# A decoder block on one core: scaling before the transpose in the second half, and reloads of merged tokens on ScalarE's DMA queue

## The chip, the cores and the metric

One core of a Trainium2 chip runs the whole kernel. The metric is the device time of one execution in microseconds (us). Three runs of the kernel before gave 3618.96, 3622.24 and 3625.21 us; their median is 3622.24 us.

## The reference, cut to what matters

The input is 512 tokens of 2048 channels, all in f32. The block computes two mixers, joins them, and ends in an expert layer:

```python
xn = rmsnorm(x, norm_mix)
proj = xn @ w_in                       # 2048 -> 10240: conv, attention and gate parts
merged = sigmoid(g_conv) * (y_conv @ w_conv_out) + sigmoid(g_attn) * (y_attn @ w_attn_out)
x = x + merged @ w_out                 # 2048 x 2048
xn = rmsnorm(x, norm_ffn)              # x * rsqrt(mean(x^2) + eps) * gain
q = xn @ peer_wq                       # queries of 8 heads, then top-16 of the keys
x = x + peer_ffn(xn, ...)              # 128 experts' rows of u and v per token
return rmsnorm(x, norm_final)
```

The change touches two places: how the merged tokens get back on chip ahead of `merged @ w_out`, and how the second `rmsnorm` is turned into the transposed operand of `xn @ peer_wq`.

## The kernel before, in words

**Halves of numbers.** TensorE multiplies f32 data as three products: every operand is split into a high half (a copy rounded by ScalarE, L133) and a low half (source minus high half, by VectorE, L134). `split` does both. `mm3` (L164 to L166) issues the three matmuls: high by high, high by low, low by high. Weights come from HBM in raw pieces of 128 x 1024 (512 KB, `whalf`, L148, on SyncE's DMA queue, called SP). Four raw buffers (`wraw`) and three buffers each of halves (`whi`, `wlo`) are in rotation.

**Token halves.** The 512 tokens are worked on as two halves of 256, h = 0 and h = 1. For each half `mixer` runs the projections, attention and convolution, then 16 blocks of the merge (block d = 0 to 15; each takes two raw pieces of `w_mix`, 24 matmuls a piece, 48 a block). Merged blocks 0 to 12 are parked in HBM (`md`), because their place on chip is still taken by the normalised input `xhi`, `xlo`. After the last projection has read that input, eight DMAs bring the parked blocks back into the same place (L345 to L348: for each of four groups of blocks a high and a low part; six DMAs of 512 KB and two of 128 KB). Blocks 13, 14 and 15 are merged after that and go there directly. `outproj` then multiplies by `w_out`, adds the residual, and takes the sum of squares of each row (L484, L485).

**The chain.** `chain` makes the second normalisation and the transposed operand of the query projection. It takes the inverse root mean square of each of two token tiles (`rms_inv`, L197 to L199, one number per token), broadcasts it along the other axis by a small matmul (L499, L500, L503: the tile `cinv`), transposes the two row tiles `x2` in eight pairs of 128-column blocks (`turn`, four transposes into one PSUM buffer of three, L208), multiplies each transposed block by gain and `cinv` into SBUF (L509, VectorE, twice a pair), and splits the pair (512 columns) into the halves `nhi`, `nlo`. For h = 1 it also reloads the 64 token columns left over from h = 0 (`ntd`, L525, L526). `queries` (L535 on) follows and needs what the chain gives.

**What sets the order.** The code is traced in program order; a list scheduler then orders each engine's instructions, taking by program order what is ready by its own estimate. [...] Beside the second half runs a gather: GpSimd fetches rows of `u` and `v` by index (L691, about 1 MB each, on its own DMA queue), and VectorE consumes them (L702, L709).

Of the kernel before, what the change touches and what calls it, by code (L numbers as in the profile page):

```python
# [8 lines left out]
F32 = mybir.dt.float32  # L9
# [3 lines left out]
AF = mybir.ActivationFunctionType  # L13
OP = mybir.AluOpType
# [4 lines left out]
P = 128  # L19
T = 512  # L20
D = 2048
KD = D // P
NH = 256
# [9 lines left out]
G0 = P + NG2  # L33
# [20 lines left out]
XKB = 3  # L54
# [12 lines left out]
PINT = 1  # L67
# [13 lines left out]
def block_kernel(ctx, tc, a, out, dbg=None):  # L81
    nc = tc.nc
# [22 lines left out]
    gffn = const.tile([P, KD], F32, name="gffn")  # L105
# [7 lines left out]
    xn2d = dram.tile([G0, D], F32, name="xn2d")  # L113
    kd = dram.tile([NPAIR, P, NH], F32, name="kd")
    vd = dram.tile([NPAIR, P, 2, P], F32, name="vd")
    md = dram.tile([2, 2, P, KD, NH], F32, name="md")
    ntd = dram.tile([2, P, KD, NH - G0], F32, name="ntd")
# [6 lines left out]
    def row():  # L124
        return late[0].tile([P, D], F32, name="row", bufs=ROWS)
# [6 lines left out]
    def split(src, hi, lo):  # L132
        nc.scalar.activation(hi, src, AF.Copy)  # L133
        nc.vector.tensor_tensor(lo, src, hi.bitcast(F32), OP.subtract)  # L134
# [24 lines left out]
    def behind(ins):  # L159

        tc.add_manual_dep(ins.ins, pe_last[0].ins.name, mybir.DependencyInfo(mybir.DependencyClass.NoSync, mybir.DependencyReason.DATA), reason="behind")
# [15 lines left out]
    def accum():  # L177
        return ps.tile([P, 512], F32, name="pj", bufs=3)
# [17 lines left out]
    def rms_inv(ss):  # L196
        nc.vector.tensor_tensor(ss[:, 0:1], ss[:, 0:1], ss[:, 1:2], OP.add)  # L197
        nc.scalar.activation(ss[:, 0:1], ss[:, 0:1], AF.Sqrt, scale=1.0 / D, bias=epst)
        nc.vector.reciprocal(ss[:, 0:1], ss[:, 0:1])  # L199
        return ss[:, 0:1]  # L200

    def turn(x2, k, pin):

        tp = accum()
        for kk in range(2):
            for tt in range(2):
                o = kk * NH + tt * P
                t = nc.tensor.transpose(tp[:, o:o + P], x2[tt][:, (k + kk) * P:(k + kk) * P + P], ident)  # L208
                if pin:
                    behind(t)  # L210
        return tp.rearrange("p (k t) -> p k t", k=2)
# [49 lines left out]
    def mixer(h, st, x):  # L261
# [67 lines left out]
        for d in range(KD):  # L329
            sg = []  # L330
            for i in (48 + d, 64 + d):
                acc = yield from project(i)
                s = mix.tile([P, NH], F32, name="sg", bufs=SG)
# [10 lines left out]
        m = st["m"] = [(st["mp"] if h == 0 else mix).tile([P, KD, NH], F32R, name=f"x{q}") for q in ("hi", "lo")]  # L344
        for k in range(0, n, 4):  # L345
            for q in range(2):
                s = slice(k, min(k + 4, n))
                nc.sync.dma_start(m[q][:, s].bitcast(F32), md[h, q, :, s])  # L348
        if h == 0:
            st["x1"] = load_x(1)  # L350
        while todo:
# [139 lines left out]
    def chain(pool, h, box, nhi, nlo, c0):  # L491

        x2 = box["x2"]
        ib = accum()
        rns = []
        for tt in range(2):
            rn = rms_inv(box["ssq"][tt])
            rb = pool.tile([P, P], F32, name="rb", bufs=2)
            nc.scalar.mul(rb, ones, rn)  # L499
            nc.tensor.matmul(ib[:, tt * P:tt * P + P], rb, ident, start=True, stop=True)  # L500
            rns.append(rn)
        inv = pool.tile([P, NH], F32, name="cinv", bufs=1)
        nc.scalar.copy(inv, ib[:, 0:NH])  # L503
        yield
        for k in range(0, KD, 2):
            tp = turn(x2, k, h == 0 and PINT)
            xk = pool.tile([P, 2, NH], F32, name="sg", bufs=1 if h == 0 else XKB)
            for j in range(2):
                nc.vector.scalar_tensor_tensor(xk[:, j], tp[:, j], gffn[:, k + j:k + j + 1], inv, OP.mult, OP.mult)  # L509
            split(xk, nhi[:, k:k + 2, c0:c0 + NH], nlo[:, k:k + 2, c0:c0 + NH])  # L510
            yield
        if h == 0:
            grow = row()
            nc.sync.dma_start(grow, a["norm_ffn"].broadcast_to([P, D]))
            yield
            for tt, rn in enumerate(rns):
                xn = x2[tt]
                nc.vector.scalar_tensor_tensor(xn, xn, rn, grow, OP.mult, OP.mult)
                stop = min(tt * P + P, G0)
                nc.sync.dma_start(xn2d[tt * P:stop], xn[0:stop - tt * P])  # L520
                yield
            nc.sync.dma_start(ntd[0], nhi[:, :, G0:].bitcast(F32))
            nc.sync.dma_start(ntd[1], nlo[:, :, G0:].bitcast(F32))
        else:
            nc.sync.dma_start(nhi[:, :, 0:c0].bitcast(F32), ntd[0])  # L525
            nc.sync.dma_start(nlo[:, :, 0:c0].bitcast(F32), ntd[1])  # L526

    def queries(pool, h, st, nhi, nlo, c0):

# [409 lines left out]
    box = [{}, {}]  # L939
    with tc.tile_pool(name="mp", bufs=1) as st["mp"]:  # L940
        for _ in mixer(0, st, load_x(0)):
            pass
        for _ in outproj(sm, 0, st["m"], box[0]):
            pass
    ahead = mixer(1, st, st["x1"])
    n0 = [mix.tile([P, KD, NH], F32R, name=n) for n in ("yhi", "ylo")]
    ch = chain(sm, 0, box[0], *n0, 0)
    for i in range(6):
        next(ahead)
# [43 lines left out]
    with tc.tile_pool(name="cp", bufs=1, side="right") as cp:  # L993
        for _ in chain(cp, 1, box[1], *st["dense_x"], ND - NH):
            pass
# [98 lines left out]
```

## Time and profile before

| | |
|---|---|
| the profiled execution's own time | 3618.28 us |
| its span | 3616.6 us |
| mean granted TensorE clock | 0.991 of full speed |
| VectorE busy | 2832.1 us (78%) |
| ScalarE busy | 1618.0 us (45%) |
| GpSimd busy | 654.8 us (18%) |
| SyncE's and ScalarE's DMA queue together (q1) | 649.38 MB, all of it issued by SP |
| GpSimd's DMA queue (q0) | 402.68 MB |

"Busy" is the share of the span in which an engine has an instruction running; matmuls overlap, so a busy TensorE is not one at its peak. In the rows further down, PE is TensorE, PEld its weight load, ACT ScalarE, DVE VectorE, SPq the issuing of DMAs by SyncE. A view by time gives for each row the start in us, the length in us, engine, line and operation, with output and inputs by the program's names; in square brackets stands how long the engine had been idle before it and what it had waited for.

### The profile page before, as it was taken

How to read it: one execution, taken by the hardware profiler on the slowest of the kernel's cores; microseconds unless marked ns; L12 is line 12 of the kernel's file. 1: busy time of each engine (PE TensorE's matmuls, PEld its weight loads, DVE VectorE, ACT ScalarE, POOL GpSimd, SP SyncE). 2: the span in 40 equal slices, each digit the busy share in tenths (PEclk: the TensorE clock that was granted, in tenths of full speed). 3: DMA queues.
4: the chain of work that ended last, by engine and by line, in shares of the span. 5: the costliest groups of instructions: out<-in, count | busy, mean ns of one | idle time of the engine just before them, and what ended most of it. 6: DMA issues, size and time to landing. Idle time of an engine off the chain costs nothing.

```text
span 3616.6 us, 63343 instructions
## 1 busy us (share of the span) xinstructions
PE 3515.7 (97%) x25347; PEld 3410.5 (94%) x25347; DVE 2832.1 (78%) x4022; ACT 1618.0 (45%) x2275; POOL 654.8 (18%) x520
## 2 busy tenths in 40 slices
PE   9999999999999999889999999999999999999998
PEld 8999998898888999779999999999999999999997
DVE  6665557559987888788999886888887888888885
ACT  5454445445555544544337763333333333333334
POOL 0000000001333222112131111221122322322220
PEclk9999999999999999999999999999999999999998
DMA  5556666654788999898888889899988988899884
GB/s 195 178 180 227 214 213 218 202 191 135 265 347 316 339 353 337 328 331 330 309 319 325 316 307 367 330 351 341 337 333 319 360 326 337 325 338 348 324 321 149
DMA packets 297815, 1056.10 MB, mean 292 GB/s; under 512 B 36464, under 2 KB 109296, under 8 KB 243568
## 3 DMA queue, kind: packets, MB, share of 16 engines
q1 hardware_dynamic: 242224, 649.38, 51.5%
q0 software_dynamic: 55296, 402.68, 28.7%
q8 instruction: 199, 3.26, 0.4%
q14 instruction: 96, 0.79, 0.1%
HBM read 999.98 MB, written 51.38 MB: 291 GB/s over the span
## 4 chain that ended last, share of the span: by engine, by line
PE 58%; DVE 4%; DMA 3%; issue 1%; ACT 1%; SPq 0%; POOL 0%; ACTq 0%; DVEq 0%
PE pj L166 10%; PE pj L164 9%; PE pj L165 9%; PE z L164 9%; PE z L165 9%; PE z L166 9%; PE pj L674 2%; DVE wlo L134 2%; DMA wraw<-in_w_in 1%; DMA row<-in_v,idx 0%; DVE row L702 0%; DMA wraw<-in_w_mix 0%; DMA gt<-gd 0%; DMA hb<-hdd 0%; DVE row L709 0%
## 5 line engine op out<-in xcount | busy, mean ns | idle before, releaser
L133 ACT ACTIVATE whi<-wraw 128x1024 fp32r<-128x1024 f32 x827 | 874.1, 1059 | 1241.2 <-PE pj L165 708.1
L134 DVE TENSOR_TENSOR wlo<-wraw,whi 128x1024 fp32r<-128x1024 f32 x827 | 1007.0, 1221 | 409.1 <-ACT whi L133 401.5
L166 PE MATMUL pj<-xhi,wlo 128*128 128x256 f32 x2560 | 720.5, 283 | 14.2 <-DVE wlo L134 13.8
L164 PE MATMUL pj<-xhi,whi 128*128 128x256 f32 x2560 | 721.8, 282 | 9.4 <-ACT whi L133 7.3
L165 PE MATMUL pj<-xlo,whi 128*128 128x256 f32 x2560 | 717.6, 281 | 0.0
L164 PE MATMUL pj<-dxhi,whi 128*128 128x320 f32 (+1 forms) x2304 | 710.3, 309 | 5.0 <-ACT whi L133 4.9
L166 PE MATMUL pj<-dxhi,wlo 128*128 128x320 f32 (+1 forms) x2304 | 703.8, 307 | 3.1 <-DVE wlo L134 2.9
L165 PE MATMUL pj<-dxlo,whi 128*128 128x320 f32 (+1 forms) x2304 | 705.4, 306 | 0.0
L164 PE MATMUL z<-ahi,whi 128*128 128x320 f32 x2048 | 632.7, 310 | 3.9 <-ACT z L193 2.9
L165 PE MATMUL z<-alo,whi 128*128 128x320 f32 x2048 | 633.1, 310 | 2.4 <-DVE alo L134 2.4
L166 PE MATMUL z<-ahi,wlo 128*128 128x320 f32 x2048 | 630.8, 310 | 1.8 <-DVE wlo L134 1.8
L166 PEld LDWEIGHTS pj<-xhi,wlo 128*128 128x128 f32 x2560 | 480.6, 188 | 24.3 <-DVE wlo L134 20.9
L164 PEld LDWEIGHTS pj<-xhi,whi 128*128 128x128 f32 x2560 | 481.6, 188 | 17.0 <-ACT whi L133 10.6
L165 PEld LDWEIGHTS pj<-xlo,whi 128*128 128x128 f32 x2560 | 481.4, 188 | 2.5 <-issue 1.4
L691 POOL DMA_INDIRECT row<-in_v,idx x192 | 288.5, 1503 | 1064.9 <-DVE row L709 412.3
L709 DVE SCALAR_TENSOR_TENSOR row<-row,gact 128x2048 f32<-128x2048 f32 x192 | 450.1, 2345 | 26.6 <-DMA row<-in_v,idx 26.3
L702 DVE SCALAR_TENSOR_TENSOR row<-row,gx 128x2048 f32<-128x2048 f32 x192 | 438.3, 2286 | 32.2 <-DMA row<-in_u,idx 32.2
L691 POOL DMA_INDIRECT row<-in_u,idx x192 | 289.7, 1509 | 859.1 <-DVE row L702 251.3
L164 PEld LDWEIGHTS pj<-dxhi,whi 128*128 128x128 f32 x2304 | 434.4, 189 | 6.3 <-ACT whi L133 5.9
L166 PEld LDWEIGHTS pj<-dxhi,wlo 128*128 128x128 f32 x2304 | 433.0, 188 | 5.1 <-DVE wlo L134 5.1
L165 PEld LDWEIGHTS pj<-dxlo,whi 128*128 128x128 f32 x2304 | 434.1, 188 | 0.0
L133 ACT ACTIVATE whi<-spare 128x1024 fp32r<-128x1024 f32 x197 | 208.9, 1060 | 422.4 <-PE z L165 257.6
(232 smaller groups left out, 4987.0 us busy)
## 6 DMA issues: line engine op xcount, KB each, us to landing
wraw<-in_w_in SPq DMA_DIRECT2D x320, 512.0 KB
wraw<-in_uT SPq DMA_DIRECT2D x187, 512.0 KB
wraw<-in_vT SPq DMA_DIRECT2D x128, 512.0 KB
spare<-in_vT SPq DMA_DIRECT2D x128, 512.0 KB
spare<-in_uT SPq DMA_DIRECT2D x69, 512.0 KB
wraw<-in_w_mix SPq DMA_DIRECT2D x64, 512.0 KB
wraw<-in_w_out SPq DMA_DIRECT2D x64, 512.0 KB
wraw<-in_wq SPq DMA_DIRECT2D x64, 512.0 KB
```

What stands on the lines that cost most here:

```text
L133: nc.scalar.activation(hi, src, AF.Copy)
L134: nc.vector.tensor_tensor(lo, src, hi.bitcast(F32), OP.subtract)
L164: nc.tensor.matmul(acc, shi, mhi, start=first, stop=False)
L165: nc.tensor.matmul(acc, shi, mlo, start=False, stop=False)
L166: pe_last[0] = nc.tensor.matmul(acc, slo, mhi, start=False, stop=last)
L674: behind(nc.tensor.matmul(gp[:, t * P:t * P + P], oh[:, t, 0], oh[:, t, 1], start=True, stop=True))
L691: ins = nc.gpsimd.indirect_dma_start(out=g, out_offset=None, in_=tab, in_offset=bass.IndirectOffsetOnAxis(ap=idx[0:np_, s:s + 1], axis=0))
L702: pin(nc.vector.scalar_tensor_tensor(g, g, 1.0, gx, OP.mult, OP.mult, accum_out=hid[:, s:s + 1]))
L709: pin(nc.vector.scalar_tensor_tensor(acc[0:np_], g, act[:, s:s + 1], acc[0:np_], OP.mult, OP.add))
```

## The change

For h = 1 three things differ. The eight reloads of `md` are issued by ScalarE instead of SyncE. The chain scales the rows first (`xs`, a new tile per token tile; ScalarE the left 1024 columns, VectorE the right 1024), transposes the scaled rows, and makes high and low half straight from PSUM, 256 columns at a time, with the gain as a per-partition number; the broadcast matmul, `cinv` and the tile `xk` are gone for h = 1. And the `ntd` reloads stand at the head of the chain in program order instead of at its end. For h = 0 nothing is changed but the nesting of the code.

```diff
-                nc.sync.dma_start(m[q][:, s].bitcast(F32), md[h, q, :, s])
+                (nc.scalar if h else nc.sync).dma_start(m[q][:, s].bitcast(F32), md[h, q, :, s])
...
     def chain(pool, h, box, nhi, nlo, c0):
         x2 = box["x2"]
+        if h:
+            nc.sync.dma_start(nhi[:, :, 0:c0].bitcast(F32), ntd[0])
+            nc.sync.dma_start(nlo[:, :, 0:c0].bitcast(F32), ntd[1])
+            xs = []
+            for tt in range(2):
+                rn = rms_inv(box["ssq"][tt])
+                xs.append(pool.tile([P, D], F32, name="xs", bufs=2))
+                nc.scalar.activation(xs[tt][:, :1024], x2[tt][:, :1024], AF.Copy, scale=rn)
+                nc.vector.tensor_scalar(xs[tt][:, 1024:], x2[tt][:, 1024:], rn, None, OP.mult)
+            yield
+            for k in range(0, KD, 2):
+                tp = turn(xs, k, False)
+                for j in range(2):
+                    g = gffn[:, k + j:k + j + 1]
+                    hi, lo = (t[:, k + j, c0:c0 + NH] for t in (nhi, nlo))
+                    nc.scalar.activation(hi, tp[:, j], AF.Copy, scale=g)
+                    nc.vector.scalar_tensor_tensor(lo, tp[:, j], g, hi.bitcast(F32), OP.mult, OP.subtract)
+                yield
+            return
         ib = accum()
...
-            tp = turn(x2, k, h == 0 and PINT)
-            xk = pool.tile([P, 2, NH], F32, name="sg", bufs=1 if h == 0 else XKB)
+            tp = turn(x2, k, PINT)
+            xk = pool.tile([P, 2, NH], F32, name="sg", bufs=1)
...
-        else:
-            nc.sync.dma_start(nhi[:, :, 0:c0].bitcast(F32), ntd[0])
-            nc.sync.dma_start(nlo[:, :, 0:c0].bitcast(F32), ntd[1])
```

## Rows read from the trace of the kernel before

**Rows 1.** The page: busy time of TensorE, its share and instructions.

```profile
PE 3515.7 (97%) x25347; PEld 3410.5 (94%) x25347; DVE 2832.1 (78%) x4022; ACT 1618.0 (45%) x2275; POOL 654.8 (18%) x520
```

**Rows 2.** Chain that ended last, 1430 to 1640: start, length, work.

```profile
1448.31 7.41 DMA xlo<-md
1455.78 15.80 DMA wraw<-in_w_mix
```

**Rows 3.** TensorE by time, the last merge blocks and the start of outproj.

```profile
1448.23 0.28 PE L164 MATMUL pj<-yhi,whi 128*128 128x256 f32 x1
...
1462.37 0.49 PE L646 MATMUL tr<-ident,eg 128*128 128x128 f32 x3
1472.71 0.58 PE L164 MATMUL pj<-yhi,whi 128*128 128x256 f32 x1 [9.86 <-ACT whi L133]
...
1478.84 1.25 PE L674 MATMUL pj<-spare 128*128 128x128 f32 x8
1479.84 0.51 PE L164 MATMUL z<-whi,xhi 128*128 128x512 f32 x1
```

**Rows 4.** A stretch: us, busy us of five engines, clock, DMA share, GB/s.

```profile
1465.00:1470.00 5.00, 0.00 (x0) 0.00 (x0) 3.29 (x7) 1.66 (x5) 0.94 (x1) 0.56 1.02 409
```

**Rows 5.** DMA issues by SP, in order of time.

```profile
1440.09 5.94 SPq L148 DMA_DIRECT2D wraw<-in_w_mix  x4
1448.31 0.33 SPq L348 DMA_DIRECT2D xlo<-md  x1
...
1454.04 0.32 SPq L348 DMA_DIRECT2D xlo<-md  x1
```

**Rows 6.** SP's waits, 1430 to 1500: waited for, us in total, times, longest.

```profile
SPq L148 <- DMA xlo<-md: 2.5, 2, 1.4
...
SPq L348 <- DMA wraw<-in_w_mix: 1.3, 1, 1.3
```

**Rows 7.** ScalarE by time, two pieces of weights.

```profile
1448.31 1.06 ACT L133 ACTIVATE whi<-wraw 128x1024 fp32r<-128x1024 f32 x1 [1.77 <-PE pj L165]
...
1476.00 1.06 ACT L133 ACTIVATE whi<-wraw 128x1024 fp32r<-128x1024 f32 x1 [2.07 <-DMA wraw<-in_w_out]
```

**Rows 8.** TensorE by time, from the end of outproj to the queries.

```profile
1583.44 0.39 PE L166 MATMUL z<-whi,xlo 128*128 128x512 f32 x1
...
1590.94 1.91 PE L208 MATMUL pj<-ident,row 128*128 128x128 f32 x8
...
1600.49 0.36 PE L164 MATMUL pj<-dxhi,whi 128*128 128x256 f32 x1 [0.16 <-DVE sg L509]
```

**Rows 9.** Stretches of the chain, columns as in rows 4.

```profile
1588.00:1590.00 2.00, 0.00 (x0) 0.00 (x0) 2.00 (x7) 1.26 (x4) 1.33 (x1) 0.62 0.83 243
...
1594.00:1596.00 2.00, 2.00 (x12) 1.59 (x11) 2.00 (x6) 1.19 (x2) 0.00 (x0) 0.68 0.95 377
```

**Rows 10.** VectorE by time in the chain.

```profile
1589.60 0.15 DVE L199 RECIPROCAL ssq<-ssq 128x1 f32<-128x1 f32 x1
1589.67 2.27 DVE L702 SCALAR_TENSOR_TENSOR row<-row,gx 128x2048 f32<-128x2048 f32 x1
...
1591.87 0.15 DVE L199 RECIPROCAL ssq<-ssq 128x1 f32<-128x1 f32 x1
1593.75 2.44 DVE L509 SCALAR_TENSOR_TENSOR sg<-pj,gffn,cinv 128x256 f32<-128x256 f32 x6 [1.73 <-ACT cinv L503]
```

**Rows 11.** Groups by line, 1430 to 1640: busy us, mean ns, idle before.

```profile
L134 DVE TENSOR_TENSOR wlo<-wraw,whi 128x1024 fp32r<-128x1024 f32 x57 | 69.2, 1221 | 31.9 <-ACT whi L133 31.8
...
L134 DVE TENSOR_TENSOR dxlo<-sg,dxhi 128x512 fp32r<-128x512 f32 x8 | 5.3, 683 | 0.1
```

**Rows 12.** Single lines elsewhere with like forms: minimum, median, maximum ns.

```profile
L900 ACT ACTIVATE row<-row,rn x3: 1135/1148/1149, 3605.7 to 3609.0; 128x1024 f32<-128x1024 f32 x2, 64x1024 f32<-64x1024 f32 x1
L902 DVE TENSOR_SCALAR row<-row,rn x3: 745/753/754, 3605.2 to 3609.0; 128x1024 f32<-128x1024 f32 x2, 64x1024 f32<-64x1024 f32 x1
L235 ACT ACTIVATE xhi<-row,gmix x16: 492/493/507, 8.1 to 19.4; 128x256 fp32r<-128x256 f32 x16
```

More of the change, by code (lines that the diff above doesn't have):

```diff
@@ L511, in chain @@
             yield
-        if h == 0:
-            grow = row()
-            nc.sync.dma_start(grow, a["norm_ffn"].broadcast_to([P, D]))
-            yield
[L516 to L523, printed above, removed]
-        else:
-            nc.sync.dma_start(nhi[:, :, 0:c0].bitcast(F32), ntd[0])
-            nc.sync.dma_start(nlo[:, :, 0:c0].bitcast(F32), ntd[1])
+        grow = row()
+        nc.sync.dma_start(grow, a["norm_ffn"].broadcast_to([P, D]))
+        yield
+        for tt, rn in enumerate(rns):
+            xn = x2[tt]
+            nc.vector.scalar_tensor_tensor(xn, xn, rn, grow, OP.mult, OP.mult)
+            stop = min(tt * P + P, G0)
+            nc.sync.dma_start(xn2d[tt * P:stop], xn[0:stop - tt * P])
+            yield
+        nc.sync.dma_start(ntd[0], nhi[:, :, G0:].bitcast(F32))
+        nc.sync.dma_start(ntd[1], nlo[:, :, G0:].bitcast(F32))
     def queries(pool, h, st, nhi, nlo, c0):
```

## The prediction

> **What bounds the kernel now.** I read the page first: TensorE is busy 97% of the span and no other engine comes near [rows 1]. So only time in which TensorE stands still, or runs slow, can be won, and both edits sit at such a place. The chain of waits shows the first: between two stretches of matmuls the end is set by a reload of merged tokens (7.41 us) and then by the load of one raw piece of `w_mix` (15.80 us) that stood behind it on SP [rows 2]. TensorE by time shows the price: it runs five pieces of the last merge blocks from 1448.23 to 1462.37, 2.83 us a piece, stands idle 9.86 us for the sixth, and then takes 1478.84 - 1472.71 = 6.13 us for it instead of 2.83 [rows 3]. The stretches say why: the granted clock falls while it waits (mean 0.56 in the stretch without a matmul, so on the lower level, 1.2 GHz, about 3 us after the idling began), with the DMA engines full at 409 GB/s [rows 4]. If the sixth piece had been there, 9.86 + 6.13 - 2.83 = 13.2 us would be saved. That is the ceiling of the first edit.
>
> The second place is the chain: TensorE does its last matmul of the output projection at 1583.44 and its first of the queries at 1600.49 [rows 8], 17 us later, with only transposes in between.
>
> **First edit: the reloads on ScalarE's queue.** Why did the sixth piece come late? SP issues strictly in order: five pieces of `w_mix` are out, then come the eight reloads from 1448.31 to 1454.36 [rows 5], then the sixth piece at 1455.78. It waited until the first reload had landed (1448.31 + 7.41 = 1455.72), and the eighth reload had waited 1.3 us for a piece of `w_mix` [rows 6]: counted in order of issue, each DMA waits for the one eight places before it. Then the piece was behind 3 MB of reloads: from 1455.72 to 1471.58, 15.86 us, the queue landed seven reloads and the piece, 5 x 512 + 2 x 128 + 512 KB = 3.4 MB, 215 GB/s. That is half of the 409 GB/s [rows 4]; the gather has the other half.
>
> With the reloads issued by ScalarE, the sixth piece has only one piece ahead of it on SP. No row shows a DMA issued by ScalarE, nor three queues at work. Bounds: the queues share evenly (a third each, 136 GB/s, 3.9 us for 512 KB), or nothing is won and the piece still lands at 1471.58. I take thirds, as two queues shared in halves. Even if the piece must still wait for the first reload, it goes out by 1455.7 and lands after at most two pieces' time, 1463.5: about when TensorE asks for it (1462.86).
>
> What the move costs is on ScalarE. It executes in order too, so the eight issues and their waits now stand in front of its other work. They become ready when TensorE has read the last of the input, at the same moment as the split of the fourth-last piece (first of block 14, 1448.31 in [rows 7]), and they are earlier in program order, so I expect all eight ahead of it. Behind them on ScalarE: that split, two more, and a sigmoid that nobody needs soon. TensorE gets to that piece at 1448.23 + 2 x 2.83 = 1453.89. Lower end of the cost: the eight places are not shared, the issues take 8 x 0.5 = 4 us, ScalarE is free at 1452.4, the high half is there at 1453.5 and the low half 1.2 us later [rows 11]: under 1 us. Upper end: the last reload waits for a landing as before, 1454.36, and that landing, with three queues instead of two, is up to 2.3 us later: 1456.7 + 1.06 + 1.22 = 1459, 5 us. I take 3.5. I take it without a fall of the clock, which needed about 3 us of idling at this place [rows 4] and 5 us after the output projection (0.62 in the stretch from 1588 [rows 9]); a fall would cost another 3.3.
>
> What is late next? The output projection needs two pieces of `w_out` and the first two reloads. In the trace the second such piece was split at 1476.00 [rows 7]; the queue had then landed some 5.9 MB since 1448.31. At two thirds of 409 GB/s the same bytes take 21.7 us: 1470.0, and the new start would be 1479.84 - 13.2 + 3.5 = 1470.1. So nearly nothing is lost there; I put 0.7 us. First edit: -13.2 + 3.5 + 0.7 = -9.0.
>
> The Trainium skill speaks against this edit: "DMA: Bandwidth & Descriptors", section "Issuing engines are not separate DMA queues", says that DMAs started by several engines run on the same 16 DMA engines and interleave, and that issuing from several saves only the sequencer's time. The full DMA share at this place [rows 4] agrees with one set of engines; whether an interleaved third goes to the piece that TensorE waits for, no row shows. Its result is the second rival.
>
> **Second edit: scale, transpose, split.** Taken from VectorE per pair: one subtraction of 512 columns (683 ns) [rows 11]. Old cost of a pair on VectorE: 2 x 2.44/6 = 0.81 [rows 10] plus 0.65 = 1.46 us. New cost: two fused operations of the same form, 0.81 us. ScalarE per pair: one of 512 columns becomes two of 256, 0.49 each alone [rows 12], less what neighbours overlap, 0.8 to 0.98. TensorE: the same 32 transposes, 0.24 each at the lower clock, 0.96 a pair (1.91 for eight [rows 8]). So a pair costs 0.85 to 0.96 instead of 1.46.
>
> But the start is later. Before, three pairs were transposed while the root was still being worked out. Now the scaling must come first: the second inverse root is ready at 1592.02, late because a gather row of 2.27 us sits between the two reciprocals [rows 10]; I leave it there. ScalarE's half row takes 1.15 us, VectorE's 0.75 [rows 12] beside it: 1593.2. First pair transposed at 1594.2, its halves done at 1595.6 (0.45 + 0.48 + 0.41 and small waits). The queries start when a PSUM buffer comes free, at the end of the sixth pair, as in [rows 8], where VectorE's L509 released it: 1595.6 + 5 x 0.85 to 0.96 = 1599.9 to 1600.4, against 1600.49. Gain: 0.1 to 0.6; I take 0.3. Ends: with the gather row out of the way -2.6; with it in the middle of the pairs +2.0; if the clock, low at 1588 and high again at about 1595 under transposes [rows 9], wakes only under the queries, +3.3 more (the size of [rows 3]). The reloads of `ntd` went out as soon as their place was free, and still do: nothing. The removed broadcast matmuls and `cinv` are inside the 1592.02 to 1593.75 that the scaling replaces [rows 10].
>
> **Sum.** -9.0 - 0.3 = -9.3 us. The profiled execution took 3618.3, 4.0 below the median of the runs, so the sum gives 3609.0 on its own base and 3612.9 on the median's. I predict 3611, between them.
>
> **Rivals** (times on the base of 3620.3, midway as well).
> - *ScalarE is not held up.* The eight places are counted for each queue alone, or the scheduler puts the splits first. For it: ScalarE is busy only 45% of the span [rows 1]. Against it: program order. The first edit gives 13.2 - 0.7: 3620.3 - 12.8 = 3607.5.
> - *The bytes bound it.* The same bytes must land before the output projection can start, whoever issues them; if the third queue takes its share from SP and not from the gather, the second `w_out` piece still lands at 1476.0, and the projection starts at about 1477 instead of 1479.84, perhaps without the slow clock: -3, 3617. For it: the DMA share of 1.02 [rows 4]; against it: the even split seen between two queues. This is the skill's rule carried through.
> - *ScalarE held until the reloads land (slower).* If ScalarE's queue takes new DMAs only as earlier ones land, at 3.9 us a piece, it is free at t, and TensorE idles from 1453.89 to t + 2.3 and pays 3.3 for the clock. Against the 13.2 of today this breaks even at t = 1461.5 and costs over 0.2% from t = 1468.7. With five of the eight waiting so, t = 1448.3 + 5 x 3.9 + 4 = 1472: +10.5, 3631. For it: the eighth reload did wait for a landing [rows 6]. Against it: on SP seven did not.
> - *The chain turns worse.* The gather row amid the pairs and the clock down: +5.3 instead of -0.3, 3616.6.
>
> **Chances.** Forecast 0.42, first rival 0.18, bytes 0.16, slower 0.12, chain 0.12. A change of 0.2% (7 us) is about what a measurement of this kernel can tell from none. Faster by more: the first rival whole and four fifths of the forecast, since a fall of the clock would take it below the bound: 0.53. Slower by more: the slower case, less its milder half, and some for an order of instructions that moves elsewhere: 0.11. Between: 0.36. The range goes from the first rival, with the lower base and 2 us for its gather row, 3603, to just above the chain case and the bytes on the median's base, 3622.
>
> **What would show it.** Right: the idle time of 9.86 us before the sixth piece is gone and its matmuls run at 2.83 us; an idle time of 2 to 5 us appears before the first piece of block 14, waiting for ScalarE's split; the reloads stand on ScalarE's queue from 1448 to about 1455; the output projection starts near 1470. In the chain: VectorE 0.8 to 0.95 us a pair, first transpose after 1593 on this clock of events, queries within a microsecond of before. Wrong: the sixth piece still lands after 1468, ScalarE's split of block 14 comes after 1461, or the transposes run at the lower clock into the queries. The later stages should be shifted only; a change of over 3 us after the queries would come from another order of instructions, which I have not priced.

## The result: slower by half a per cent, and the profile after

The changed kernel took 3640.47 us (median; 3639.17 to 3646.62), the kernel before 3622.84 us beside it (3618.96 to 3625.21). The ratio is 1.0054, 95% interval 1.0042 to 1.0066: 17.6 us more, where 9.3 less was predicted. The profiled execution took 3639.24 us (span 3637.5, mean granted clock 0.987 against 0.991).

Both kernels split the same 1024 weight pieces in the same sequence (ScalarE, L133), so the start of the i-th split says how far each is (the piece numbers below count from 0 in this sequence). This table gives by how much a profile fell behind the profile of the kernel before in each part, in us. The last row but one is the edit of the chain alone, the last the edit of the reloads alone (both are experiments below).

| | up to the last projection (1438) | to outproj, under way (1512) | to its end (1573) | chain, to the queries (1625) | queries, first dense pieces (1785) | to 1813 | to 2005 | to the end |
|---|---|---|---|---|---|---|---|---|
| after | 4.3 | 0.6 | 0.0 | 3.4 | 0.1 | 6.2 | 4.5 | 2.0 |
| after, run again | 5.9 | 3.5 | 0.0 | 3.5 | 0.8 | 8.9 | 1.9 | 4.6 |
| chain alone | 7.9 | -2.8 | 0.0 | 2.6 | 0.0 | 0.0 | -0.4 | -0.3 |
| reloads alone | 4.0 | 3.7 | 0.0 | 0.2 | -0.2 | 0.0 | 5.2 | -0.6 |

The first column is not the change. Up to the reloads every engine has the same instructions in the same order in all of these kernels, and the execution of the kernel before that was profiled lies 4.6 us below the median of its runs. The other columns of the first row add to 16.8 us, near the 17.6 of the medians. They name three places: the first edit won nothing (predicted: 9.0 won), the chain lost 3.4 (0.3 won), and 12.8 us were lost behind the chain, where no line was changed, 10.7 of them between 1785 and 2005.

**The first edit.** ScalarE by time, with its DMA issues (ACTq). This answers to [rows 5, 7]:

```profile
1453.03 0.34 ACTq L348 DMA_DIRECT2D xlo<-md  x1
...
1456.71 0.52 ACTq L348 DMA_DIRECT2D xhi<-md  x1
1459.40 0.33 ACTq L348 DMA_DIRECT2D xlo<-md  x1
1459.78 2.95 ACT L133 ACTIVATE whi<-wraw 128x1024 fp32r<-128x1024 f32 x3 [5.97 <-DMA xhi<-md]
1462.63 0.40 ACT L133 ACTIVATE xhi<-sg 128x256 fp32r<-128x256 f32 x1
1466.03 1.06 ACT L133 ACTIVATE whi<-wraw 128x1024 fp32r<-128x1024 f32 x1 [2.99 <-issue]
...
1479.08 0.42 ACT L133 ACTIVATE xhi<-sg 128x256 fp32r<-128x256 f32 x1 [0.71 <-DVE sg L317]
1479.40 2.93 ACT L133 ACTIVATE whi<-wraw 128x1024 fp32r<-128x1024 f32 x3
```

The eighth reload waits for an earlier one to land, and everything behind it on ScalarE waits too: 6.75 us from 1453.03 to the split at 1459.78. The eight places of the prediction are eight completion semaphores (101 to 108 in the trace), which the program hands to the DMAs of SP and of ScalarE in turn, counted over both; GpSimd has its own. Here the first reload has 108, SP's sixth piece 101, the next six reloads 102 to 107, and the eighth 108 again: it goes out at 1459.40, when the first has landed (1459.38). SP waits in the same way: its third piece of `w_out` takes 103 and goes out at 1465.43, when the third reload has landed (1465.38). The sixth piece of `w_mix` is indeed there in time. It landed at 1457.93, which is 1453.6 when the 4.3 us of the first column are taken off, 18 us earlier than in the kernel before (1471.58); its split, 1466.03 or 1461.7, came 10 us earlier and did not wait for it. TensorE, answering to [rows 3]:

```profile
1460.89 0.54 PE L164 MATMUL pj<-yhi,whi 128*128 128x256 f32 x1 [2.12 <-ACT whi L133]
...
1480.49 1.22 PE L164 MATMUL z<-whi,xhi 128*128 128x512 f32 x2 [4.16 <-ACT whi L133]
...
1482.78 0.80 PE L165 MATMUL z<-wlo,xhi 128*128 128x512 f32 x1 [1.07 <-DVE wlo L134]
```

The idle 9.86 us are gone; three others have come: 2.12 us before block 14, and 4.16 and 1.07 us at the start of the output projection. The 4.16 us end with ScalarE's first split of `w_out` (1479.40 above), which stands behind the high half of the last merge block, and that waited for VectorE (`sg`, L317). VectorE shows what it did ahead of L317 and of the low halves:

```profile
1472.19 2.28 DVE L717 SCALAR_TENSOR_TENSOR row<-row,gx 128x2048 f32<-128x2048 f32 x1
...
1474.40 0.48 DVE L672 TENSOR_SCALAR spare<-iota,egT 128x128 f32<-128x128 f32 x2
...
1478.63 0.42 DVE L317 TENSOR_TENSOR sg<-sg 128x256 f32<-128x256 f32 x1
1478.96 2.28 DVE L717 SCALAR_TENSOR_TENSOR row<-row,gx 128x2048 f32<-128x2048 f32 x1
...
1481.17 0.42 DVE L134 TENSOR_TENSOR xlo<-sg,xhi 128x256 fp32r<-128x256 f32 x1
1481.51 3.49 DVE L134 TENSOR_TENSOR wlo<-wraw,whi 128x1024 fp32r<-128x1024 f32 x3
```

Between two rows of the gather it makes one-hot planes for the gates (L672, L677: planes of 128 x 128 that hold a value where an index equals the column's number, from which TensorE makes the gate table of the experts) and only then finishes the last merge block (L317) and the low halves of `w_out`. The kernel before made the first of these planes here:

```profile
1463.40 0.48 DVE L657 TENSOR_SCALAR spare<-iota,egT 128x128 f32<-128x128 f32 x2 [0.42 <-ACT egT L648]
...
1466.00 2.28 DVE L702 SCALAR_TENSOR_TENSOR row<-row,gx 128x2048 f32<-128x2048 f32 x1
```

That is inside the old idle time (1462.86 to 1472.71). The old stall was not empty: 2.6 us of one-hot work and a row of 2.3 us were done under it. With the stall gone they stand on the path. Stretches of the changed kernel, columns as in [rows 4]:

```profile
1445.00:1450.00 5.00, 5.00 (x35) 5.00 (x35) 3.65 (x4) 1.33 (x2) 0.94 (x1) 0.77 0.83 296
...
1460.00:1465.00 5.00, 3.92 (x19) 3.63 (x20) 4.13 (x6) 3.04 (x4) 0.44 (x1) 0.66 1.02 424
...
1475.00:1480.00 5.00, 1.33 (x8) 0.95 (x7) 5.00 (x19) 3.50 (x9) 0.69 (x1) 0.80 1.01 411
1480.00:1485.00 5.00, 3.44 (x7) 2.34 (x8) 5.00 (x6) 2.33 (x3) 0.00 (x0) 0.50 0.36 125
1485.00:1490.00 5.00, 5.00 (x16) 3.94 (x15) 1.23 (x1) 1.06 (x1) 0.00 (x0) 0.67 0.72 234
```

VectorE is busy 10.00 of 10 us from 1475 to 1485. And the granted clock fell twice, at block 14 (0.66) and at the start of the output projection (0.50, 0.67), where the kernel before had only the one fall. Of the 13.2 us of the old stall 7.4 came back as idle time; with 0.6 lost in sum, 6.4 are left for slower matmuls (by difference). Not all of these belong to the change: the clock was also low ahead of the first reload (0.89 from 1440 to 1445, 0.77 from 1445 to 1450). By these two rows some 3.4 us ran at half speed, which costs about 1.7 us (an estimate). In the second profile of the changed kernel both stretches have 1.00.

**The chain.** TensorE and VectorE, answering to [rows 8, 10]:

```profile
1596.03 0.90 PE L208 MATMUL pj<-ident,xs 128*128 128x128 f32 x3 [7.27 <-ACT xs L501]
1598.85 2.18 PE L208 MATMUL pj<-ident,xs 128*128 128x128 f32 x9 [1.92 <-ACT xs L501]
1601.96 2.79 PE L208 MATMUL pj<-ident,xs 128*128 128x128 f32 x12 [0.93 <-DVE dxlo L510]
1605.47 1.94 PE L208 MATMUL pj<-ident,xs 128*128 128x128 f32 x8 [0.71 <-DVE dxlo L510]
```

```profile
1594.60 2.27 DVE L717 SCALAR_TENSOR_TENSOR row<-row,gx 128x2048 f32<-128x2048 f32 x1
...
1596.80 0.75 DVE L502 TENSOR_SCALAR xs<-row,ssq 128x1024 f32<-128x1024 f32 x1
1597.46 0.16 DVE L199 RECIPROCAL ssq<-ssq 128x1 f32<-128x1 f32 x1
...
1600.30 0.48 DVE L510 SCALAR_TENSOR_TENSOR dxlo<-pj,gffn,dxhi 128x256 fp32r<-128x256 f32 x1 [1.90 <-ACT dxhi L509]
...
1608.98 0.48 DVE L510 SCALAR_TENSOR_TENSOR dxlo<-pj,gffn,dxhi 128x256 fp32r<-128x256 f32 x1
```

The first token tile's half row (0.75 us) went in between the gather row and the second reciprocal, and the eight pairs took 1600.30 to 1609.4, 1.14 us each. The clock, columns as in [rows 9]:

```profile
1602.00:1604.00 2.00, 2.00 (x10) 1.93 (x11) 1.49 (x4) 1.03 (x4) 0.00 (x0) 0.50 1.05 389
1608.00:1610.00 2.00, 2.00 (x12) 2.00 (x11) 1.85 (x4) 0.76 (x2) 0.00 (x0) 0.50 0.73 303
1610.00:1612.00 2.00, 2.00 (x14) 2.00 (x14) 1.67 (x2) 0.06 (x1) 0.00 (x0) 0.71 0.00 0
```

All transposes and the first matmuls of the queries ran at the lower level (1.2 GHz); before, it was left at about 1595 [rows 9].

**Behind the queries.** The chain of waits of the changed kernel, from 1790 (start, length, work), and SP's issues:

```profile
1794.84 2.22 DVE row L717 x2
1797.07 0.48 SPq L769
...
1798.29 13.27 DMA wraw<-in_uT
1811.65 1.07 ACT whi L133
1812.76 0.63 PE pj L164
```

```profile
1797.07 1.12 SPq L769 DMA_DIRECT2D gx<-xn2d  x2
1798.29 4.18 SPq L148 DMA_DIRECT2D wraw<-in_uT  x3
```

SP's order is another one here: the gather's second input tile (`gx`, L769) is reloaded ahead of three weight pieces, and cannot go before VectorE has read the old one for the last time (L717, until 1797). In the kernel before one piece more was ahead of these two DMAs. TensorE stands still 3.20 us at 1798 (for a low half) and 2.45 us at 1812 (for this DMA), and loses the clock again (matmuls 0.27 us apart until about 1816, 0.15 after). The list scheduler made this order. From the end of the chain on, the two edits together give other orders on every engine; each alone keeps nearly the old one.

### The profile page after: what moved, and what is told of

Its sections match the earlier page's. It is cut to its first block, busy times and chain, and to the rows that moved or that the text cites. A ratio compares the mean times of both kernels' runs of the same rounds, so it can differ in the third digit from the quotient of the medians.

```text
span 3637.5 us, 63333 instructions
## 1 busy us (share of the span) xinstructions
PE 3524.8 (97%) x25343; PEld 3417.2 (94%) x25343; DVE 2828.2 (78%) x4016; ACT 1620.1 (45%) x2282; POOL 651.4 (18%) x520
## 4 chain that ended last, share of the span: by engine, by line
PE 62%; DVE 4%; DMA 3%; issue 2%; ACT 1%; SPq 0%; POOL 0%; ACTq 0%; DVEq 0%; POOLq 0%
PE pj L166 11%; PE pj L164 10%; PE pj L165 10%; PE z L164 9%; PE z L165 9%; PE z L166 9%; PE pj L689 2%; DVE wlo L134 1%; DVE row L717 1%; DMA row<-in_u,idx 1%; DMA wraw<-in_uT 1%; PE z L440 1%; DMA gt<-gd 0%; ACT whi L133 0%; DMA hb<-hdd 0%
## 5 line engine op out<-in xcount | busy, mean ns | idle before, releaser
L133 ACT ACTIVATE whi<-wraw 128x1024 fp32r<-128x1024 f32 x827 | 873.8, 1059 | 1293.6 <-PE pj L165 750.1
L717 DVE SCALAR_TENSOR_TENSOR row<-row,gx 128x2048 f32<-128x2048 f32 x192 | 438.5, 2287 | 41.5 <-DMA row<-in_u,idx 41.5
L133 ACT ACTIVATE whi<-spare 128x1024 fp32r<-128x1024 f32 x197 | 208.9, 1060 | 427.6 <-PE z L165 263.4
```

The source lines that it names most:

```text
L717: pin(nc.vector.scalar_tensor_tensor(g, g, 1.0, gx, OP.mult, OP.mult, accum_out=hid[:, s:s + 1]))
```

## Experiments

Each is named by its ratio to the kernel before and its interval. "Part" means a column of the table above.

**The reloads alone**, run twice; the trace read here is the second's.

```diff
-                nc.sync.dma_start(m[q][:, s].bitcast(F32), md[h, q, :, s])
+                (nc.scalar if h else nc.sync).dma_start(m[q][:, s].bitcast(F32), md[h, q, :, s])
```

> Only the first edit: the reloads of merged tokens are issued by ScalarE, the chain is the old one. The planner's order of all engines is the old one again from the queries on. Theory (the first edit by itself is neutral: the 13 us won on the sixth piece are lost again to ScalarE's hold, about 2 us of idling and a fall of the clock, and to an idle time of 4 us with a second fall of the clock before outproj; the rest of the 18 us comes from the chain, 3 us, and from another order of instructions in the queries and the first dense chunks, about 10 us): 3620 to 3627, within 0.2% of before; the sixth piece without a wait, TensorE idle about 2 us before the first piece of block 14 and 4 us before outproj. Rival (the whole loss is made by ScalarE's hold and what it drags behind it): 3636 to 3642.

> The first edit alone once more, for a profile that can be read. Theory: the sixth piece without a wait, TensorE idle about 2 us before block 14 and 3 to 5 us before outproj with the clock on its lower level after both, outproj's end within 1.5 us of the old distance from the last projection; later stages as before; +0.1 to +0.2%. Rival: outproj ends 5 us or more earlier and the time goes later.

Ratios 1.0016 (1.0007 to 1.0024) and 1.0009 (1.0000 to 1.0018). The second's trace shows waits at the same three places, 5.78 (about 2 was expected), 4.16 and 1.06 us, with 3.7 us lost in its part, where at most 1.5 was expected, and 5.2 us between 1813 and 2005, where nothing was expected. The median of the first, 3628.62 us, lies 1.6 above its range. So the first edit is at best worth nothing, without the chain.

**The chain alone** (the diff of the chain; reloads on SP).

> Only the second edit: the new chain, the reloads stay on SyncE's queue. Theory: the chain is 3 us slower because TensorE has no work until the scaled rows are there, its clock stays on the lower level through all transposes and into the queries; later stages keep nearly the old order: 3624 to 3629, +0.1%. Rival (the chain carries the whole loss, its changed order later too): 3636 to 3642. Second rival (as forecast, the chain is neutral): 3619 to 3623.

1.0004 (0.9994 to 1.0014), 3623.07 us, on the border of the theory and the second rival. In the trace its part loses 2.6 us, as the theory said, and the later parts nothing. The two edits alone add to 5 to 7 us by their ratios; together they cost 18 to 20. The difference lies behind the queries.

**The chain alone, with 24 idle transposes ahead of it**, to keep the clock up.

```diff
             xs = []
+            for k in range(0, 12, 2):
+                turn(x2, k, False)
```

> As the run before (second edit only), with 24 more transposes of the unscaled rows, whose results nobody reads, put ahead of the chain's own, so that TensorE is at work while the rows are scaled. If the low clock is the chain's loss: granted clock back at the upper level before the chain's own transposes end, a pair in 0.8 to 0.9 us, queries at full speed from their first matmul, 3 to 5 us less than the run before it. Rival (the pace is set by ScalarE and VectorE, not by the clock): within 1.5 us of it.

1.0031 (1.0019 to 1.0042), slower than without the transposes, which neither side expected. This tells nothing of the clock: the transposes needed only the residual sums and ran at 1586 to 1588, and TensorE then stood idle 4.15 us all the same; the part of the chain lost 3.1. But the run is one more case of another order behind: 12 us were lost there.

**Both edits again, and with 8 and 16 idle transposes at the end of the chain** (they change the scheduler's times a little).

```diff
                 yield
+            for k in range(0, 4, 2):        # 8; range(0, 8, 2) for 16
+                turn(xs, k, False)
             return
```

> The changed kernel once more, on one chip with the runs beside it. Theory (order of instructions in the queries and the first dense chunks costs about 10 us, the chain 3, the reloads nothing): +0.35 to +0.5% against before, idle times over 2 us at the same places of the dense stage as in its first profile (pieces around 1800 and 1920). Rival (much of the 18 us was the execution-to-execution spread of the part ahead of the change, whose order is the old one): under +0.25%.

> Both edits, and after the chain's last pair 8 more transposes that nobody reads (at most 8 x 0.24 = 1.9 us of TensorE). From the eighth dense unit on the planner gives all engines the order that it gives the changed kernel. Theory (that order costs 10 us): as the changed kernel or 2 us more, +0.35 to +0.55%. Rival (the order is harmless): under +0.25%.

> Both edits, and 16 such transposes, 2 us more work than the run before it. The planner now falls back on the old kernel's order from about the fourth dense chunk on, and gives a third order before that. Theory (order): 4 to 10 us less than the run before it, although it does more: +0.1 to +0.3% against before. Rival (the front alone sets the time): 2 us more than the run before it.

1.0050 (1.0035 to 1.0064), 1.0050 (1.0037 to 1.0063), 1.0039 (1.0026 to 1.0052). The loss is reproduced. The run with 16 was to be 4 to 10 us faster than the one with 8 by the theory, 2 us slower by the rival; it was 1.3 us faster (medians 3638.63 and 3639.94), which neither says and the spread covers. In the part to 1813 these three lost 8.9, 2.6 and 8.7 us. The second profile of the changed kernel stood still at 1803 and 1820 as the first had, but not near 1920. In the third, 24 transposes ran back to back, and the clock did not rise under them:

```profile
1607.08 5.67 PE L208 MATMUL pj<-ident,xs 128*128 128x128 f32 x24 [0.71 <-DVE dxlo L510]
1612.40 0.56 PE L164 MATMUL pj<-dxhi,whi 128*128 128x256 f32 x1
```

```profile
1608.70:1610.70 2.00, 1.94 (x10) 1.54 (x9) 1.47 (x4) 1.31 (x3) 0.00 (x0) 0.50 1.00 420
1610.70:1612.70 2.00, 2.00 (x11) 2.00 (x10) 2.00 (x2) 0.00 (x0) 0.00 (x0) 0.50 0.35 143
1612.70:1614.70 2.00, 2.00 (x18) 2.00 (x17) 2.00 (x3) 0.00 (x0) 0.00 (x0) 0.97 0.00 0
```

**Both edits, the gather's reload issued by GpSimd.** TensorE, VectorE and ScalarE keep the changed kernel's order instruction for instruction; only SP's loses these two DMAs.

```diff
-                nc.sync.dma_start(t[r * NG2:r * NG2 + NG2], xn2d[P:G0])
+                nc.gpsimd.dma_start(t[r * NG2:r * NG2 + NG2], xn2d[P:G0])
```

> Both edits as they are, but the two reloads of the gather's second input tile (gx, 64 rows each) are issued by GpSimd instead of SyncE. TensorE, VectorE and ScalarE keep the order of the changed kernel instruction for instruction; on SyncE only these two DMAs are gone from ahead of three weight pieces. Theory (the place of those two reloads on SyncE holds the weight pieces back until VectorE has read gx for the last time, near 1797): the loss between the 538th and the 545th piece of the second part, 6.2 and 9.0 us in the two profiles of both edits, falls to under 1.5 us; the idle times of TensorE of 3.2 and 2.5 to 5.1 us near 1800 to 1820 go, the time falls from 3640-3644 to about 3634, ratio to the kernel before about 1.003. Rival 1 (the pieces are late because the transfers themselves are slow there): the idle times stay, 3641. Rival 2 (VectorE's low halves are late behind the rows of the gather): the first idle time of 3.2 us stays and only the second goes, about 3638.

1.0045 (1.0030 to 1.0060), 3639.46 us: by the time and the waits the second rival, not my theory. In the part to 1813 it lost 3.2 us, where the two runs of both edits lost 6.2 and 8.9. The wait for the DMA is gone; the other stays:

```profile
1804.82 0.63 PE L166 MATMUL pj<-dxhi,wlo 128*128 128x320 f32 x1 [3.20 <-DVE wlo L134]
```

VectorE, in the same order as in the changed kernel, takes two rows of the gather ahead of that low half; the kernel before took one, and TensorE waited 0.53 and 0.69 us. In the run with both edits here:

```profile
1798.01 2.27 DVE L717 SCALAR_TENSOR_TENSOR row<-row,gx 128x2048 f32<-128x2048 f32 x1
...
1801.34 2.27 DVE L717 SCALAR_TENSOR_TENSOR row<-row,gx 128x2048 f32<-128x2048 f32 x1
...
1803.55 2.35 DVE L134 TENSOR_TENSOR wlo<-wraw,whi 128x1024 fp32r<-128x1024 f32 x2
```

The two waits have different standing. All eight profiles in which VectorE takes two rows there (both edits and their variants, the chain with 24 transposes ahead, and two runs below) show TensorE waiting 2.75 to 3.20 us for it; in the seven others it waits 0.69 us at most. The wait for the piece does not go with SP's order so well. With the two reloads of `gx` ahead of three pieces it was 2.45, 5.07 and 2.29 us in three profiles and at most 1.0 us in four others. With 8 idle transposes, where SP has that order, it was 0.67 us:

```profile
1805.26 0.42 PE L166 MATMUL pj<-dxhi,wlo 128*128 128x320 f32 x1 [2.75 <-DVE wlo L134]
1818.00 0.41 PE L164 MATMUL pj<-dxhi,whi 128*128 128x320 f32 x1 [0.67 <-ACT whi L133]
```

With the old order it was 2.11 and 3.83 us in two of the runs with groups below. The 3.2 us of this run lie between the 2.6 and the 8.9 of runs that keep SP's order. So the run does not show that the place of these two DMAs makes the piece late, only that the wait was absent once without it. About 3 us of the loss go with VectorE's order, which was not tried alone; the other 0 to 6 us are a late piece, whose cause is open.

**The reloads in four groups on ScalarE** (old chain), the first where they were, each other one after a merge block.

```diff
-        for k in range(0, n, 4):
+        def reload(k):
...
+        else:
+            reload(groups.pop(0))
         while todo:
             yield from merge(*todo.pop(0), m)
+            if groups and h:
+                reload(groups.pop(0))
             yield
```

> Old chain; the reloads go out on ScalarE in four groups: the first where it stands, the others after each of the last three merge blocks in program order, so that the split of block 14 is not behind all of them. If ScalarE's hold is what eats the gain: no idle time over 1 us before block 14 and no fall of the clock there, outproj 3 to 6 us earlier than in the first run of this set. Rival (the order of one-hot work on VectorE and ScalarE ahead of outproj decides): the idle time before outproj stays at 3 us or more and outproj starts no earlier.

1.0013 (1.0002 to 1.0023). ScalarE is still held (5.14 us before its third split after the first reload), but TensorE no longer feels it (0.37 us of idle time before block 14), and the output projection starts 7.3 us earlier than before (1472.53), after 3.04 us of waiting for ScalarE. The theory was right on the hold and the start, the rival on the wait before the projection. By 1512 the gain is 1.1 us. So the hold alone was not what ate the first edit's gain.

**The one-hot work later.** It starts at a step of the output projection. A control has the old reloads and this start four steps later; two more runs have the groups, with the start four and two steps later:

```diff
-                if not (todo and unit >= GATES_AT):     # GATES_AT is 100
+                if not (todo and unit >= 104):          # 102, 101 in other runs
```

> Control: the kernel before with only the start of the gates four steps later; no edit of the change. The idle time of about 9.9 us before the sixth w_mix piece stays, and the end of the output projection is within 2 us of the kernel before. In its order on SyncE the gather's two reloads stand ahead of three weight pieces, as in the changed kernel. Theory of that place: 5 to 9 us lost between about 1785 and 1820, time 3627 to 3632. If that place were harmless: 3621 to 3624.

> Old chain; the reloads of merged tokens on ScalarE's queue in four groups, each group after a merge block; and the one-hot work of the gates starts four steps of the output projection later. In the order of instructions ScalarE then splits ten pieces of w_out without one-hot work between them, and the gather's reloads stand behind one weight piece on SyncE as in the kernel before. Theory (the gain of the first edit was eaten by one-hot work ahead of the first splits of w_out and by the fall of the clock that followed): no idle time over 1.5 us before the first matmul of the output projection, which starts 9 to 12 us earlier than in the kernel before; at the end of the output projection 8 to 11 us are won; the time is 3612 to 3616. Rival (bytes: the pieces of w_out land no earlier): the projection starts at most 3 us earlier, TensorE waits for a DMA of w_out, time 3619 to 3622. If the delayed gates cost later: won at the end of the output projection, lost behind it.

> As the run with the reloads in groups and the gates four steps later, but two steps instead of four; ScalarE splits six pieces of w_out ahead of the one-hot work. Its order on SyncE has the gather's two reloads ahead of three weight pieces, as in the changed kernel. Theory: 8 to 11 us won at the end of the output projection as with four steps, then 5 to 9 us lost between about 1775 and 1815, time 3619 to 3624. If the place of the reloads on SyncE were harmless, the same time as with four steps, 3612 to 3616; if the one-hot order were not what ate the first edit's gain, 1 us won at the end of the output projection as with the groups alone, 3625 to 3632.

The control: 1.0080 (1.0067 to 1.0093), far worse than expected. TensorE waits 14.55 us for the sixth piece (from 1467.5). One row of the gather falls under its first three us, and then hardly anything:

```profile
1470.00:1475.00 5.00, 0.00 (x0) 0.00 (x0) 0.19 (x2) 0.00 (x0) 0.94 (x1) 0.60 1.02 419
1475.00:1480.00 5.00, 0.00 (x0) 0.00 (x0) 0.00 (x0) 0.00 (x0) 0.00 (x0) 0.50 1.01 415
```

With the groups it is 1.0022 (1.0011 to 1.0032): 20 us less than the control. From the last projection to the queries' first pieces (the 484th piece) the control takes 182.8 us, the groups 168.9: 13.9 us, of which 9.4 lie before 1512 and 3.0 in the chain. The ceiling of the control, reckoned as in the prediction, is 14.55 + 6.07 - 2.83 = 17.8 us, since its sixth piece took 6.07 us of matmuls. So against a kernel whose stall covers no one-hot work the reload's new place wins most of the ceiling. But the kernel before takes 169.1. Up to 1512 the groups with four steps won 12.8 us, and paid 7.9 back by the end of the output projection, where the one-hot matmuls then stand: 4.9 won there, where 8 to 11 were expected. With two steps: 1.0035 (1.0022 to 1.0048), 9.6 won, 7.3 paid back, 4.6 lost from 1625 to 1785, and 3.9 lost near 1800, where SP and VectorE have the changed kernel's order; the control, with that order too, lost 4.5 near 1800, and the run with four steps, with the old order, 0.0. Both times lie above their ranges.

**One step later**, with the reloads held as in the change and in groups.

> Old chain; the eight reloads on ScalarE's queue as in the change (not in groups); the one-hot work of the gates starts one step of the output projection later, so that ScalarE splits the first four pieces of w_out ahead of it. The gather's reloads stand behind one weight piece on SyncE, as in the kernel before. Theory (the stall of the kernel before had covered one-hot work of VectorE and ScalarE; with the stall gone it stands ahead of the first splits of w_out; the hold of ScalarE costs 4 to 6 us besides): the idle time of 5 to 6 us before block 14 stays, the 4.2 and 1.1 us before the output projection go; from the last projection to the queries it takes 163 to 169 us instead of 173.0 with the reloads alone and 169.1 in the kernel before; nothing is lost near 1790 to 1815; time 3616 to 3624. Rival (the time from the last projection to the queries is set by the sum of VectorE's work there, so moving the one-hot work wins nothing): 171 to 174 us, time 3625 to 3630.

> As the run beside it, but with the reloads in four groups, one after each merge block, so that ScalarE is not held. Theory: no idle time over 1.5 us before block 14; from the last projection to the queries 158 to 164 us; time 3612 to 3619, faster than the kernel before. Rival (VectorE's sum sets it): 168 to 171 us, as with the gates four steps later (168.9), time 3622 to 3628.

1.0008 (0.9999 to 1.0017) and 1.0025 (1.0016 to 1.0034). From the last projection to the 484th piece they take 173.9 and 167.4 us. The first is what the rival said: with the hold, moving the one-hot work wins nothing (173.0 where it is not moved); TensorE then waits 2.42 and 2.12 us at the start of the output projection, for VectorE behind two rows of the gather. Taking away the hold alone wins nothing either (173.5 with the groups and the one-hot work in its old place). Without both it is 167.4. So each covers the other, and some 6 us come only when both are out of the way; these are single executions, and three profiles with both edits and the same hold (the changed kernel twice, and the run with the gather's reload on GpSimd) took 172.5 to 175.4. The 167.4 us are 1.7 better than the kernel before, nearer the rival's 168 than my 158 to 164. ScalarE then waits for something else:

```profile
1475.77 2.24 ACT L133 ACTIVATE whi<-wraw 128x1024 fp32r<-128x1024 f32 x2
1481.09 1.06 ACT L133 ACTIVATE whi<-wraw 128x1024 fp32r<-128x1024 f32 x1 [3.07 <-DMA wraw<-in_w_out]
1484.82 1.06 ACT L133 ACTIVATE whi<-wraw 128x1024 fp32r<-128x1024 f32 x1 [2.68 <-DMA wraw<-in_w_out]
```

With hold and one-hot work out of the way it waits for the pieces of `w_out` themselves. TensorE does not: it waits 3.24 us before the output projection (1476.86), for ScalarE behind the last merge block and a row of the gather on VectorE, and from there to 1512 never more than 0.53 us. Near 1800 this kernel lost 5.2 us although SP has the old order: there a raw piece took 12.05 us to land, and TensorE waited 3.83 us for it. So the old order is not enough to be safe. No version beat the kernel before.

## Why the prediction was wrong

By the table the forecast of -9.3 us became +16.8. Of this difference 9.6 us lie in the first edit, 3.7 in the chain, and 12.8 behind the chain, which the prediction put at nothing.

**The ceiling of 13.2 us was taken for a loss of TensorE alone.** This is the step that failed in the first edit. "If the sixth piece had been there, 9.86 + 6.13 - 2.83 = 13.2 us would be saved" holds if the other engines do nothing in the stall that TensorE will need. [rows 4] showed otherwise: VectorE was busy 3.29 of 5 us in it, and the prediction used that row only for the clock and the DMA rate. The one-hot work and the gather row under it came onto the path. "So nearly nothing is lost there; I put 0.7 us" was therefore wrong: the output projection started at 1480.49, that is 1476.2 on the clock of the kernel before, and not near 1470. Against the control, whose stall covers no one-hot work, 9.4 us are there by 1512 and 13.9 by the queries, of a ceiling of 17.8. That the one-hot work alone took the gain is not shown: moved to later, it is paid for later (7.9 of 12.8 us), and with the hold in place moving it wins nothing. Nor do that work (4.9 us) and the hold (2.1) add up to the 13.2: some 6 us are left, of which the slower matmuls after the new waits are a part.

**The hold was named and about rightly sized, its clock was not.** 3.5 us were put for it, bounds under 1 to 5, without a fall of the clock. Measured: 2.12 us of idle time in the changed kernel, 1.8 to 5.8 in the six others with the same reloads; and in the changed kernel the clock fell (0.66) with 2.12 us of idle time. The eighth reload waited for a landing, as the upper bound had it. The first rival's "counted for each queue alone" did not hold: the eight semaphores are counted over SP's and ScalarE's DMAs together.

**The bytes** were a rival that no run bears out for TensorE. The Trainium skill's "DMA: Bandwidth & Descriptors", section "Issuing engines are not separate DMA queues", has all issuers share the same 16 engines. This case's trace agrees: the DMA share is 1.02 at 424 GB/s with three issuers as it was 1.02 at 409 with two [rows 4]. The start that this rival gave for the projection, about 1477, was nearly met (1476.2), but by chance: the wait there was for ScalarE and VectorE and not for a landing, and the first piece of `w_out` had landed at about 1470, well before its split at 1479.40. Once hold and one-hot work are gone, ScalarE waits 5.8 us for `w_out`, but TensorE does not wait for it. Which queue a piece stands in still counted: the sixth piece landed 18 us earlier.

**The chain: -0.3 predicted, 2.6 to 3.5 measured** with either form of the reloads. The start was later (the first tile's scaling ahead of the second reciprocal, not priced), a pair took 1.14 us instead of 0.85 to 0.96, and the clock stayed low into the queries: the end of the range that I priced at 3.3 and did not take. The trace divides the 3.4 us of the changed kernel about in half. The first matmul of the queries starts at 1607.06, or 1602.16 less the 4.9 us it was behind at 1573, 1.7 us later than in [rows 8]; the next 17 matmuls start 0.21 us apart instead of 0.12, some 1.6 us more. How much of the first half belongs to the clock too is open: no run kept it up. (The prediction also says that three pairs were transposed ahead of the root; [rows 8] shows eight transposes, two pairs. The sum does not use it.)

**"The later stages should be shifted only."** They were not: 12.8 us, the largest single term, came from there, 10.7 of them between 1785 and 2005, and the prediction said that it had not priced another order of instructions. The 6.2 us near 1800 are mainly a wait of 3.20 us for VectorE, which goes with its new order in every profile that has it, and one of 2.45 us for a late piece, whose cause is open. The 4.5 us between 1813 and 2005 are not settled: TensorE waits 3.83 us at 1920 for a one-hot plane, but not when the same kernel ran again (1.9 us lost), and the reloads alone lost 5.2 us there as well. The last 2.0 us were not looked into.

## What to carry to other kernels

A stall of the engine that bounds the kernel is worth its length only if nothing that this engine will need soon is done under it: list what the other engines execute inside the stall, and ask where that work will stand once the stall is gone. DMAs issued from ScalarE held ScalarE's later work here while one of them waited for an earlier one to land, because the program gave both the same semaphore (6.75 us); in groups they still held it (5.14 us), but where TensorE hardly felt it (0.37 us). So choose the place of such DMAs by what stands behind them. Where a scheduler orders the whole program by its own estimates, a local edit can reorder everything behind it; run each edit alone and both together before crediting or blaming either.

## What the runs showed that I had not expected

- The same instructions in the same order took between 0.5 us less and 9.0 us more up to the last projection than in the first profile (14 profiles). A difference of some us between two single executions is no finding; only steps between aligned points, or medians with intervals, are.
- The wait for the sixth piece was 9.86 us in the kernel before and 14.55 in the control, with the same order of DMAs at that place.
- TensorE's clock stayed at 0.50 through 5.67 us of transposes without a gap, and was back at 0.97 within the first two us of the queries. In the kernel before it had risen under transposes at about 1595 [rows 9]. Whether the transposes or the queries' matmuls brought it back is not shown.
